# The samples' steps of a two-branch mixer as a chain of their own, with a distance behind each step

## The chip, the cores and the metric

The kernel runs on one core of a Trainium2 chip. The metric is the device time of one execution in microseconds (us). Lower is better. Each time quoted is a median of runs, or one profiled execution where that is said.

The engines are named as in the profile: PE (matrix multiplications), DVE and ACT (elementwise work), POOL, and SP, which issues most of the loads.

## The reference

One layer of a hybrid decoder is computed for a prompt of 1024 tokens and for 8 samples of one token each. They share the weights.

```python
h = rmsnorm(x, norm_gain)
q, k, v, gla_g, a_lr, u, pool_g, xq, xg, merge = split(h @ w_in)
# A: gated linear attention, 4 heads (dk 128, dv 256), chunks of 64, per-head rmsnorm
br_gla  = rmsnorm(gla_chunked(q, k, v, log_sigmoid(a_lr @ w_a2 + b_a) / 16, S0)) * silu(gla_g)
# B: trailing means over 2, 4, 8 and 16 rows, minus the row, linear map of each group, scale
br_pool = multiscale_pool(u, hist) * silu(pool_g)
# C: cross attention of 4 heads (256 wide) into 256 memory tokens
br_x    = cross_attn(xq, mem_k, mem_v) * silu(xg)
merged  = sum_n sigmoid(merge_n) * (branch_n @ w_branch_n)
y       = rmsnorm(x + merged @ w_out, final_gain)
```

For the prompt the memory keys and values come from `mem @ w_mk` and `mem @ w_mv`, and the attention state starts at zero. For each of the 8 samples the keys, the values, the attention state (128 x 256 per head) and the last 15 pooling rows are read from their own caches. Everything is float32, so a large product is split into a high and a low part and made of three matmuls (`mm3`).

## The kernel before

**The large product.** `h @ w_in` is cut into 40 pairs of column blocks, and each pair is computed by seven products of half-size blocks. One call of `run_product` is such a product: 24 matmuls of 128x258 into `px` banks of PSUM. `seq` is the list of the 280 products, and the text numbers them from 1. `prepare` makes the weights' operands (names `a11`, `a12`, `a22`, `s1` to `s4`, each with an `h` and an `l` half) three products ahead: ACT writes the high half (L221), DVE the low half (L222), and DVE also makes sums of raw blocks (`ws<-raw`, L293). The raw blocks are loaded by SP (L284).

**The fill.** After each product `emit` calls `fill`, which adds steps of other work to the same queues. A `Stream` hands out steps of a generator so that the work done, in units written in the `yield`s, keeps up with a line from its first to its last slot. A slot number rises by 2 with each product. The first stream (`mix`) holds the cross attention and then the gated linear attention, from product 15 to 179; the second (`pool_steps`) the pooling, up to product 249.

**Two kinds of steps.** The long sequences (the prompt) of the cross attention: `cross_memory` (M) transposes a head's keys; `cross_scores` (S) makes scores, a maximum, exponentials and a scaling; `cross_weights` (W) transposes the weights and splits them; `cross_values` (V) multiplies by the values. Of the linear attention: `gla_gates` (GG, a long chain on ACT and DVE), `gla_within` (GW, whose result is split into `akvh` and `akvl`), `gla_recur` (R, L867 its last matmul) and `gla_out` (GO, L896).

The samples have generators of their own. `cross_sample` for each head: `cross_rows` transposes the queries and writes them to DRAM; `fetch` loads two samples' keys (`kc`) and their query, spread over all partitions (`qb`); DVE multiplies and sums them (L683, four per fetch, four fetches); the scores `sc` are transposed (L695), softmax, transposed again (L707, copied to `pm`, L708); then two halves of values (`vc`) are loaded and multiplied (L721), and the result transposed (L731). `gla_sample` for each head: rows, gates, two halves of states (`s0`, `vb`) that are fetched, updated, stored and multiplied (L952), and a normalised result (L967).

In the kernel before each sample generator is drawn from inside the long sequences' generator (`yield next(samples, 0)`) at fixed places: five offers per chunk of the cross attention, four per chunk of the linear attention. A small number in a `yield` (0.5) is there to use up an offer.

**What fixes the order.** PE and SP run in the order in which the code issues instructions. On ACT, DVE and POOL a scheduler places them when the kernel is built; on the chip each engine then runs in that fixed order. Steps of a fill use two PSUM banks (`PZ`, tile `pz`) in turn: a step that takes a bank waits until whatever reads the step before the last has finished. `V` is a ring of four buffers for the samples' loads, and one key fetch takes three of them.

Of the kernel before, what the change touches and what calls it, by code (L numbers as in the profile page):

```python
# [9 lines left out]
F32 = mybir.dt.float32  # L10
# [5 lines left out]
ALU = mybir.AluOpType  # L16
# [20 lines left out]
NR = 14  # L37
WORK_A, WORK_B = 493.0, 108.0
WINDOWS = (2, 4, 8, 16)
# [8 lines left out]
def trunk_kernel(ctx: ExitStack, tc: tile.TileContext,  # L48
# [589 lines left out]
    def cross_values(h, c):  # L638
# [9 lines left out]
        nc.gpsimd.dma_start(out=mix_chunk(2, h, c), in_=g)  # L648

    def cross_rows(h):  # L650

        xs = tiny(16, "xs").rearrange("p (i b) -> p i b", i=2)
        nc.vector.tensor_scalar(xs, smp_of(S_XQ + 2 * h, 2), 1.0 / 16.0, None, op0=ALU.mult)
        t = PZ()
        for i in range(2):
            nc.tensor.transpose(t[:NS, i * P:(i + 1) * P], xs[:, i], ident)
        qn = R([DV], name="qn")
        nc.scalar.activation(qn[:NS], t[:NS, :DV], AF.Copy)
        nc.gpsimd.dma_start(out=xq_scr[h], in_=qn[:NS])

    def cross_sample(h):

        if h == 0:
            cross_rows(0)
# [11 lines left out]
        kcs, qb = fetch(0)  # L676
        yield 0.5
        yield 0.5
        for b2 in range(4):
            for bb in range(2):  # L680
                b, kc = 2 * b2 + bb, kcs[bb]
                for a in range(2):
                    nc.vector.tensor_tensor_reduce(kc[:, a, :], kc[:, a, :], qb[:, bb, :],  # L683
                                                   scale=1.0, scalar=0.0, op0=ALU.mult, op1=ALU.add,
                                                   accum_out=sc[:, a * NS + b:a * NS + b + 1])
# [6 lines left out]
        yield 0.5  # L692
        t = PZ()
# [8 lines left out]
        nc.vector.tensor_scalar(p, p, sm, None, op0=ALU.mult)  # L702
        yield 1.2
        yield 0.5
        t = PZ()
# [7 lines left out]
        vc = own_values(0)  # L713
        yield 1.2
        yield 0.5
        cs = R([2, DV], name="cs")
        for i in range(2):
            t = PZ()
            for a in range(2):
                for j in range(4):  # L720
                    nc.tensor.matmul(t[32 * j:32 * j + 32, :DV], lhsT=pm[:, a, 4 * i + j, :], rhs=vc[j][:, a, :],  # L721
                                     start=a == 0, stop=a == 1)
            nc.scalar.activation(cs[:, i], t[:, :DV], AF.Copy)
            vc = own_values(1) if i == 0 else None
            yield 1.2
            yield 0.5
            yield 0.5
        t = PZ()
# [3 lines left out]
        for d in range(2):  # L732
            nc.vector.tensor_copy(perm8(brs[2][:, 2 * h + d]), column0(t, d))
        yield 1.2

    def cross_steps():
# [12 lines left out]

        samples = chain_of(cross_sample(h) for h in range(NH))  # L750
        cross_load(0)
        cross_memory(0)
        cross_fetch(0, 0)
        yield 2
        cross_queries(0, 0)
        cross_fetch(0, 1)
        for s in range(16 + 2):
            if s < 16:
                scores(s)
                yield 3  # L760
                if s + 1 < 16:
                    cross_queries(*divmod(s + 1, 4))
# [9 lines left out]
            if s >= 1:  # L772
                yield next(samples, 0)
            if s % 4 == 3 and s < 15:
                memory(s + 1)
                yield 2
            if 0 <= s - 1 < 16:
                weights(s - 1)
                yield 1.7
            for _ in range(3):  # L780
                if s >= 1:
                    yield next(samples, 0)
        yield from samples

    def chain_of(gens):
        for g in gens:
            yield from g

# [121 lines left out]
    def gla_sample(h):  # L910

        if h == 0:
            gla_rows(0)
            yield 1
        t = PZ()
# [5 lines left out]
        nc.vector.tensor_scalar(qm[:, :, 0], smp_of(S_Q + h)[:, 0], DK ** -0.5, None, op0=ALU.mult)  # L921
        yield 2
        ks = smp_of(S_K + h)[:, 0]
# [17 lines left out]
        for i in range(2):  # L941
            fetched = [fetch(4 * i + b0) for b0 in (0, 2)]
            yield 1
            yield 0.5
            s0 = []
            for b0 in (0, 2):
                s0.append(states(4 * i + b0, *fetched[b0 // 2]))
                yield 1.5
            yield 0.5
            t = PZ()  # L950
# [4 lines left out]
            nc.scalar.activation(t[:, :DV], t[:, :DV], AF.Square, accum_out=sq[:, i:i + 1])  # L955
            yield 1
# [5 lines left out]
        yield 1  # L962
        yield 0.5
        t = PZ()
# [6 lines left out]
        yield 1.2  # L971

    def gla_steps():
        samples = chain_of(gla_sample(h) for h in range(NH))
        N = 16
        gla_load(0, 0)
        gla_load(0, 1)
        gla_gates(0, 0)
        gla_values(0, 0)
        yield 5  # L980
        for n in range(N + 1):
            h, c = divmod(n, 4)
            ph, pc = divmod(n - 1, 4)
            if n + 1 < N:
                gla_gates(*divmod(n + 1, 4))
                yield 5
            if n < N:
                gla_within(h, 2 * c)
                yield 2
            if n > 0:  # L990
                gla_recur(ph, 2 * pc + 1)
                yield 2
                yield next(samples, 0)
            if n < N:
                gla_within(h, 2 * c + 1)
                yield 2
                yield next(samples, 0)
# [5 lines left out]
                yield 2  # L1003
            if n > 0:
                gla_out(ph, pc)
                yield 2
            for _ in range(2):
                if n >= 1:
                    yield next(samples, 0)
        yield from samples  # L1010

# [3 lines left out]
    def pool_steps():  # L1015
# [5 lines left out]

        fetched = group_fetch(0)
        for g, w in enumerate(WINDOWS):
            raw, hist = fetched
# [15 lines left out]
            nc.gpsimd.dma_start(out=o_pool_s[:, HIST - 1, g * DV:(g + 1) * DV], in_=hr[:NS])  # L1040
            yield 3
            diffs, us_ = {}, {}
# [60 lines left out]
            yield 3 + g  # L1103
            for c in range(4):
# [4 lines left out]
                mixed(c)  # L1109
                yield 4 + g if c < 3 else 2  # L1110
            t = PZ()
# [4 lines left out]
            nc.gpsimd.dma_start(out=o_pool_p[:, g * DV:(g + 1) * DV], in_=hr[:HIST])  # L1116
            yield 1

# [3 lines left out]
    def mix():  # L1122
        yield from cross_steps()
        yield from gla_steps()

    class Stream:


        def __init__(self, steps, work, first, last):
            self.steps, self.work, self.first, self.last, self.done, self.over = steps, work, first, last, 0, False  # L1130

        def run(self, slot):
            while self.done < self.work * (slot - self.first) / (self.last - self.first):
                cost = next(self.steps, None)
                if cost is None:
                    self.over = True
                    break
                self.done += cost

        def rest(self):  # L1140
            self.done += sum(self.steps)
# [3 lines left out]
    state = {"slot": 0}  # L1145

    def fill():

        s = state["slot"] = state["slot"] + 2
        next(memory, None)  # L1150
# [272 lines left out]
```

## Time and profile before

| | |
|---|---|
| median of 3 runs | 1486.27 us (1485.35 to 1486.29) |
| the profiled execution | 1486.76 us, span 1485.1 us |
| mean granted clock of PE | 0.99 |
| PE busy | 1449.9 us, 98% of the span |
| DVE busy | 880.6 us, 59% |
| ACT busy | 679.1 us, 46% |

The span runs from the first to the last instruction of the profile; the execution's time adds 1.7 us around it. A group of instructions is shown as line, engine, operation, output tile <- input tiles, shape and count. A bracket "[1.96 <-ACT xqsh L224]" behind an instruction says that its engine stood idle for 1.96 us before it and that ACT's `xqsh` of line 224 ended that. "PEclk" is the share of full speed that PE's clock was granted.

### The profile page before, as it was taken

To read this page: it belongs to the slowest core of one execution; us is meant where nothing else is said; L and a number is where in the kernel's file an instruction comes from. 1 tells how busy PE (TensorE), PEld (TensorE's weight loads), DVE (VectorE), ACT (ScalarE), POOL (GpSimd) and SP (SyncE) were. 2 spreads that over 40 slices of the span, in tenths; PEclk is the share of its full clock that TensorE was granted. 3 is DMA by queue.
4 is the path that set the end of the run, shared out by engine and by line. 5 is a ranking of instruction groups with operands and counts; after the bars stand their busy time and mean duration, and the time that the engine had idled before them with its cause. 6 is when DMAs were issued, how large, how long until landed. Compare 5 with 4: busy or idle time off the path is not lost.

```text
span 1485.1 us, 28245 instructions
## 1 busy us (share of the span) xinstructions
PE 1449.9 (98%) x10881; PEld 1386.6 (93%) x10881; DVE 880.6 (59%) x2020; ACT 679.1 (46%) x1564; POOL 160.1 (11%) x297
## 2 busy tenths in 40 slices
PE   7999999999999999999999999999999999999997
PEld 6798999989899999999989999999999999999786
DVE  5824757555577666666756578685672434554435
ACT  5623444344466665655654444444472332333212
POOL 3121101011111111110111110110010000000000
PEclk9999999999999999999999999999999999999999
DMA  8443566555545354553444455554595677632502
GB/s 297 153 166 128 186 212 201 182 196 178 195 145 173 108 185 146 172 159 125 160 162 134 155 183 165 165 190 145 190 302 160 223 251 248 226 100 93 199 29 86
DMA packets 181714, 255.25 MB, mean 172 GB/s; under 512 B 20412, under 2 KB 134740, under 8 KB 181572
## 3 DMA queue, kind: packets, MB, share of 16 engines
q1 hardware_dynamic: 159772, 179.61, 39.1%
q0 software_dynamic: 21664, 73.59, 13.1%
q8 instruction: 85, 1.39, 0.4%
q14 instruction: 49, 0.40, 0.1%
q10 hardware_dynamic: 144, 0.26, 0.0%
HBM read 176.27 MB, written 77.59 MB: 171 GB/s over the span
## 4 chain that ended last, share of the span: by engine, by line
PE 87%; DMA 5%; DVE 4%; ACT 2%; issue 1%; SPq 0%; DVEq 0%; POOLq 0%; ACTq 0%
PE px L240 24%; PE px L241 24%; PE px L242 24%; PE pz L391 3%; DMA qb<-xqs 2%; PE pz L240 2%; PE pz L242 2%; PE pz L241 2%; DMA raw<-in_w_in_dram 1%; DVE kc L683 1%; DMA x<-in_x_prompt_dram 1%; PE pz L867 1%; PE px L428 1%; PE pz L849 1%; DMA vc<-in_cache_mem_v_dram 1%
## 5 line engine op out<-in xcount | busy, mean ns | idle before, releaser
L240 PE MATMUL px<-bh,wbh 128*128 128x384 f32 (+1 forms) x576 | 184.2, 320 | 0.0
L241 PE MATMUL px<-bl,wbh 128*128 128x384 f32 (+1 forms) x576 | 184.1, 320 | 0.0
L242 PE MATMUL px<-bh,wbl 128*128 128x384 f32 (+1 forms) x576 | 184.0, 319 | 0.0
L482 ACT ACTIVATE r<-px 128x258 f32<-128x258 f32 x240 | 90.1, 377 | 44.3 <-PE px L242 42.9
L241 PEld LDWEIGHTS px<-bl,wbh 128*128 128x128 f32 x576 | 108.4, 188 | 0.0
L242 PEld LDWEIGHTS px<-bh,wbl 128*128 128x128 f32 x576 | 108.3, 188 | 0.0
L240 PEld LDWEIGHTS px<-bh,wbh 128*128 128x128 f32 x576 | 108.2, 188 | 0.0
L240 PE MATMUL px<-ot,s2h 128*128 128x258 f32 x320 | 93.4, 292 | 0.0
L240 PE MATMUL px<-o,a12h 128*128 128x258 f32 x320 | 93.3, 292 | 0.0
L240 PE MATMUL px<-ot,a22h 128*128 128x258 f32 x320 | 93.2, 291 | 0.0
L240 PE MATMUL px<-o,s4h 128*128 128x258 f32 x320 | 92.9, 290 | 0.3 <-DVE c L547 0.3
L240 PE MATMUL px<-ot,s1h 128*128 128x258 f32 x320 | 93.1, 291 | 0.0
L240 PE MATMUL px<-o,a11h 128*128 128x258 f32 x320 | 92.9, 290 | 0.0
L240 PE MATMUL px<-ot,s3h 128*128 128x258 f32 x320 | 92.7, 290 | 0.0
L242 PE MATMUL px<-ot,s2l 128*128 128x258 f32 x320 | 91.4, 286 | 0.0
L241 PE MATMUL px<-o,a12h 128*128 128x258 f32 x320 | 91.2, 285 | 0.0
L242 PE MATMUL px<-o,a12l 128*128 128x258 f32 x320 | 91.0, 284 | 0.0
L241 PE MATMUL px<-ot,s2h 128*128 128x258 f32 x320 | 91.0, 284 | 0.0
L241 PE MATMUL px<-ot,a22h 128*128 128x258 f32 x320 | 91.0, 284 | 0.0
L242 PE MATMUL px<-o,a11l 128*128 128x258 f32 x320 | 90.2, 282 | 0.8 <-DVE a11l L222 0.8
L242 PE MATMUL px<-ot,a22l 128*128 128x258 f32 x320 | 90.8, 284 | 0.0
L242 PE MATMUL px<-ot,s1l 128*128 128x258 f32 x320 | 90.7, 284 | 0.0
(457 smaller groups left out, 4577.5 us busy)
## 6 DMA issues: line engine op xcount, KB each, us to landing
raw<-in_w_in_dram SPq DMA_DIRECT2D x80, 512.0 KB, 3.9
msc<-c POOLq DMA_DIRECT2D x24, 516.0 KB, 4.4
brsc<-c POOLq DMA_DIRECT2D x24, 516.0 KB, 4.3
sig<-msc SPq DMA_DIRECT2D x24, 516.0 KB, 6.0
mix<-mixsc SPq DMA_DIRECT2D x48, 256.0 KB, 4.5
brr<-brsc SPq DMA_DIRECT2D x48, 256.0 KB, 5.4
wbr<-in_w_branch_dram SPq DMA_DIRECT2D x24, 512.0 KB, 6.2
acc<-sig POOLq DMA_DIRECT2D x16, 516.0 KB, 5.2
```

Of the source, the lines that this page charges most:

```text
L240: nc.tensor.matmul(out, lhsT=lh, rhs=rh, start=start, stop=False, skip_group_check=more)
L241: nc.tensor.matmul(out, lhsT=lh, rhs=rl, start=False, stop=False, skip_group_check=more)
L242: nc.tensor.matmul(out, lhsT=ll, rhs=rh, start=False, stop=stop, skip_group_check=more)
L391: nc.tensor.matmul(t[:, :DV], lhsT=memT[k // 2][:, k % 2, a * P:(a + 1) * P], rhs=raw[k // 2][:, k % 2], start=k == 0, stop=k == NK - 1)
L428: nc.tensor.transpose(t[:, j * P:(j + 1) * P], xt[j][:, k * P:(k + 1) * P], ident)
L482: nc.scalar.activation(r, acc[c][:, :QT], AF.Copy)
L683: nc.vector.tensor_tensor_reduce(kc[:, a, :], kc[:, a, :], qb[:, bb, :], scale=1.0, scalar=0.0, op0=ALU.mult, op1=ALU.add, accum_out=sc[:, ...
L849: nc.tensor.matmul(t[0:64, 0:P], lhsT=ki[:, 0:64], rhs=qi, start=True, stop=True)
L867: nc.tensor.matmul(to, lhsT=kiqi[:, 1, cs], rhs=st, start=False, stop=True)
```

## The change

- The samples' chain becomes an object, `Paced`, made once from all eight generators (four heads of cross attention, then four of the linear attention). `mix` offers it a place after every step of the long sequences, and draws what is left at the end.
- Every `yield` now gives two numbers: the work, and a distance. Behind a long step the distance is counted in products before the stream's next step (`Stream.ready`). Behind a sample's step it is 0, 1 or 2 and becomes 0, 2 or 3 slots before the chain's next step (`Paced.ready`); since slots rise by 2, that is no, one or two products. The yields of 0.5 are gone, merged into their neighbours.
- `Stream.run` starts no further step once two PSUM banks have been taken in this fill (`count["pz"]`).
- In `cross_sample` the scaling of the queries is a step of its own (`cross_scaled`), with a tile `xsq` of its own, ahead of `cross_rows`.
- In `cross_steps` the first scores are a fill of their own, two products after the first `cross_memory`; the first loads of the linear attention are issued at s = 15 and its first gates at s = 16, inside the cross attention. In `gla_steps` the last R and in `pool_steps` the first steps get a distance.
- `WORK_A` is 497 instead of 493, for the changed sum of the work.

The core of the diff:

```diff
+    count = {"pz": 0, "slot": 0, "rest": False}
     def PZ():
+        count["pz"] += 1
...
         kcs, qb = fetch(0)
-        yield 0.5
-        yield 0.5
+        yield 0.5, 2
         for b2 in range(4):
...
             if b2 < 3:
                 kcs, qb = fetch(b2 + 1)
-                yield 1.2
+                yield 2.2, 2
             elif h + 1 < NH:
+                cross_scaled(h + 1)
+                yield 1, 1
                 cross_rows(h + 1)
-            yield 1
-        yield 0.5
+        yield 1, 1
...
-        yield 1.2
-        yield 0.5
+        yield 1.7, 2
...
         cross_fetch(0, 0)
-        yield 2
         cross_queries(0, 0)
         cross_fetch(0, 1)
+        yield 2, 2
         for s in range(16 + 2):
             if s < 16:
                 scores(s)
-                yield 3
+                yield 3, int(s < 2)
...
-            if s >= 1:
-                yield next(samples, 0)
             if 0 <= s - 2:
                 values(s - 2)
-                yield 1.7
+                yield 1.7, 0
...
+    class Paced:
+        def __init__(self, gens):
+            self.gen, self.ready, self.over = (v for g in gens for v in g), 0, False
+        def step(self):
+            if self.over or (count["slot"] < self.ready and not count["rest"]):
+                return 0, 0
+            v = next(self.gen, None)
+            if v is None:
+                self.over = True
+                return 0, 0
+            self.ready = count["slot"] + (0, 2, 3)[v[1]]
+            return v[0], 0
...
     def mix():
-        yield from cross_steps()
-        yield from gla_steps()
+        for steps in (cross_steps(), gla_steps()):
+            for v in steps:
+                yield v
+                yield samples.step()
+        while not samples.over:
+            yield samples.step()[0], 1
...
         def run(self, slot):
-            while self.done < self.work * (slot - self.first) / (self.last - self.first):
-                cost = next(self.steps, None)
+            used = count["pz"]
+            while (self.done < self.work * (slot - self.first) / (self.last - self.first)
+                   and slot >= self.ready and count["pz"] < used + 2):
+                v = next(self.steps, None)
...
-                self.done += cost
+                self.done += v[0]
+                self.ready = slot + 2 * v[1]
```

Three places show how the instructions move. Lines of the changed kernel are 3 to 12 higher than those of the kernel before (a step's L601 is its L604); `px` rows are the products, `pz` rows the fill's steps.

PE at product 15, the start of the cross attention, before: M's transposes (`mkv`), then the first S (`mkTh` are the keys, `xqsh` and `xq` the two halves of the queries).

```order
L241 MATMUL px<-ot_933,a22h 128x258
L242 MATMUL px<-ot_932,a22l 128x258
L601 MATMUL pz<-ident,mkv 128x128 x4
L240 MATMUL pz<-mkTh,xqsh 128x256
L241 MATMUL pz<-mkTl,xqsh 128x256
L242 MATMUL pz<-mkTh,xq 128x256
```

The same place in the changed kernel:

```order
L244 MATMUL px<-ot_933,a22h 128x258
L245 MATMUL px<-ot_932,a22l 128x258
L604 MATMUL pz<-ident,mkv 128x128 x4
L243 MATMUL px<-o_502,a12h 128x258
L244 MATMUL px<-o_503,a12h 128x258
L245 MATMUL px<-o_502,a12l 128x258
```

Two products (16 and 17) now stand between M and the first S.

DVE where the fourth head's keys are split (`mkTl`, `mkv`), before: the key products `kc` of the samples' third head stand around the split.

```order
L222 TENSOR_TENSOR a12l<-raw,a12h 128x512
L222 TENSOR_TENSOR s2l<-ws,s2h 128x512
L683 ISA kc,sc<-kc,qb 128x256
L683 ISA sc 128x1
L222 TENSOR_TENSOR mkTl<-pz,mkTh 128x512
L222 TENSOR_TENSOR mkv<-mkv,mvsh 128x512
L556 TENSOR_TENSOR c_3628<-px,r_3426 128x258
```

The same split in the changed kernel:

```order
L708 RECIPROCAL sm<-sm 8x1
L709 TENSOR_SCALAR ps<-ps,sm 8x256
L225 TENSOR_TENSOR s3l<-ws,s3h 128x512
L296 TENSOR_TENSOR ws<-raw 128x512
L225 TENSOR_TENSOR mkTl<-pz,mkTh 128x512
L225 TENSOR_TENSOR mkv<-mkv,mvsh 128x512
L533 TENSOR_TENSOR c_3373<-px,r_3231 128x258
```

No key products stand near it any more; the samples are at their second head's softmax there.

PE at product 177, the end of the linear attention, before: a sample's multiplication by its states, then the last GO, one product after the last R.

```order
L241 MATMUL px<-o_507,a12h 128x258
L242 MATMUL px<-o_506,a12l 128x258
L952 MATMUL pz<-s_9808,pm 32x256 x2
L952 MATMUL pz<-s_9812,pm 32x256 x2
L896 MATMUL pz<-ident,on 128x128 x4
L240 MATMUL px<-ot_655,s2h 128x258
```

The last GO in the changed kernel, at product 179, two products after the last R:

```order
L244 MATMUL px<-ot_707,s1h 128x258
L245 MATMUL px<-ot_706,s1l 128x258
L908 MATMUL pz<-ident,on 128x128 x4
L243 MATMUL px<-ot_773,s3h 128x258
L244 MATMUL px<-ot_774,s3h 128x258
```

No sample's step is left here; the samples end at product 165.

More of the change, by code (lines that the diff above doesn't have):

```diff
@@ L37 @@
 NR = 14
-WORK_A, WORK_B = 493.0, 108.0
+WORK_A, WORK_B = 497.0, 108.0
 WINDOWS = (2, 4, 8, 16)
@@ L648, in cross_values, with cross_scaled @@
         nc.gpsimd.dma_start(out=mix_chunk(2, h, c), in_=g)
+    def cross_scaled(h):
+        xs = wk.tile([P, 16], F32, tag="xsq", name="xsq", bufs=2).rearrange("p (i b) -> p i b", i=2)
+        nc.vector.tensor_scalar(xs, smp_of(S_XQ + 2 * h, 2), 1.0 / 16.0, None, op0=ALU.mult)
+        cross["xs", h] = xs
     def cross_rows(h):
-        xs = tiny(16, "xs").rearrange("p (i b) -> p i b", i=2)
-        nc.vector.tensor_scalar(xs, smp_of(S_XQ + 2 * h, 2), 1.0 / 16.0, None, op0=ALU.mult)
+        xs = cross["xs", h]
         t = PZ()
@@ L663, in cross_sample @@
         if h == 0:
+            cross_scaled(0)
+            yield 1, 1
             cross_rows(0)
-            yield 1.2
-            yield 0.5
-            yield 0.5
+            yield 1.2, 2
         sc = wk.tile([P, 16], F32, tag="sc", name="sc", bufs=2)
@@ L713, in cross_sample @@
         vc = own_values(0)
-        yield 1.2
-        yield 0.5
+        yield 1.7, 2
         cs = R([2, DV], name="cs")
@@ L724, in cross_sample @@
             vc = own_values(1) if i == 0 else None
-            yield 1.2
-            yield 0.5
-            yield 0.5
+            yield 2.2, 2
         t = PZ()
@@ L733, in cross_sample @@
             nc.vector.tensor_copy(perm8(brs[2][:, 2 * h + d]), column0(t, d))
-        yield 1.2
+        yield 1.2, 0
     def cross_steps():
@@ L748, in values @@
             cross_values(n // 4, n % 4)
-        samples = chain_of(cross_sample(h) for h in range(NH))
         cross_load(0)
@@ L766, in cross_steps @@
                 cross_load(s // 4 + 1)
-            if s >= 1:
-                yield next(samples, 0)
             if 0 <= s - 2:
                 values(s - 2)
-                yield 1.7
-            if s >= 1:
-                yield next(samples, 0)
+                yield 1.7, 0
             if s % 4 == 3 and s < 15:
                 memory(s + 1)
-                yield 2
+                yield 2, 0
+            if s == 15:
+                gla_load(0, 0)
+                gla_load(0, 1)
+            if s == 16:
+                gla_gates(0, 0)
+                yield 5, 0
             if 0 <= s - 1 < 16:
                 weights(s - 1)
[L779 to L787, printed above, removed]
+                yield 1.7, int(s >= 15)
+    class Paced:
[10 more added lines that the diff above has]
+            return v[0], 0
     gla = {}
@@ L913, in gla_sample @@
             gla_rows(0)
-            yield 1
+            yield 1, 1
         t = PZ()
@@ L921, in gla_sample @@
         nc.vector.tensor_scalar(qm[:, :, 0], smp_of(S_Q + h)[:, 0], DK ** -0.5, None, op0=ALU.mult)
-        yield 2
+        yield 2, 1
         ks = smp_of(S_K + h)[:, 0]
@@ L942, in gla_sample @@
             fetched = [fetch(4 * i + b0) for b0 in (0, 2)]
-            yield 1
-            yield 0.5
+            yield 1.5, 2
             s0 = []
@@ L947, in gla_sample @@
                 s0.append(states(4 * i + b0, *fetched[b0 // 2]))
-                yield 1.5
-            yield 0.5
+                yield 2, 1
             t = PZ()
@@ L955, in gla_sample @@
             nc.scalar.activation(t[:, :DV], t[:, :DV], AF.Square, accum_out=sq[:, i:i + 1])
-            yield 1
+            yield 1, 0
         if h + 1 < NH:
@@ L961, in gla_sample @@
             nc.scalar.activation(os_[:, i], os_[:, i], AF.Copy, scale=r[:, i:i + 1])
-        yield 1
-        yield 0.5
+        yield 1.5, 2
         t = PZ()
@@ L970, in gla_sample @@
                                     op0=ALU.mult)
-        yield 1.2
+        yield 1.2, 0
+    samples = Paced([f(h) for f in (cross_sample, gla_sample) for h in range(NH)])
     def gla_steps():
-        samples = chain_of(gla_sample(h) for h in range(NH))
         N = 16
-        gla_load(0, 0)
-        gla_load(0, 1)
-        gla_gates(0, 0)
         gla_values(0, 0)
-        yield 5
         for n in range(N + 1):
@@ L985, in gla_steps @@
                 gla_gates(*divmod(n + 1, 4))
-                yield 5
+                yield 5, 0
             if n < N:
                 gla_within(h, 2 * c)
-                yield 2
+                yield 2, 0
             if n > 0:
                 gla_recur(ph, 2 * pc + 1)
-                yield 2
-                yield next(samples, 0)
+                yield 2, 0 if n < N else 2
             if n < N:
                 gla_within(h, 2 * c + 1)
-                yield 2
-                yield next(samples, 0)
+                yield 2, 0
                 if n + 2 < N:
@@ L1002, in gla_steps @@
                 gla_recur(h, 2 * c)
-                yield 2
+                yield 2, 0
             if n > 0:
                 gla_out(ph, pc)
[L1006 to L1010, printed above, removed]
+                yield 2, 0
     HALO = 16
@@ L1022, in pool_steps @@
         fetched = group_fetch(0)
+        yield (0.5), 2
         for g, w in enumerate(WINDOWS):
@@ L1109, in pool_steps @@
                 mixed(c)
-                yield 4 + g if c < 3 else 2
+                yield (4 + g if c < 3 else 2), 0
             t = PZ()
@@ L1116, in pool_steps @@
             nc.gpsimd.dma_start(out=o_pool_p[:, g * DV:(g + 1) * DV], in_=hr[:HIST])
-            yield 1
+            yield (1), 0
     memory = mem_units()
     def mix():
-        yield from cross_steps()
-        yield from gla_steps()
+        for steps in (cross_steps(), gla_steps()):
[4 more added lines that the diff above has]
+            yield samples.step()[0], 1
     class Stream:
         def __init__(self, steps, work, first, last):
-            self.steps, self.work, self.first, self.last, self.done, self.over = steps, work, first, last, 0, False
+            self.steps, self.work, self.first, self.last = steps, work, first, last
+            self.done, self.ready, self.over = 0, 0, False
         def run(self, slot):
-            while self.done < self.work * (slot - self.first) / (self.last - self.first):
-                cost = next(self.steps, None)
-                if cost is None:
+            used = count["pz"]
+            while (self.done < self.work * (slot - self.first) / (self.last - self.first)
+                   and slot >= self.ready and count["pz"] < used + 2):
+                v = next(self.steps, None)
+                if v is None:
                     self.over = True
                     break
-                self.done += cost
+                self.done += v[0]
+                self.ready = slot + 2 * v[1]
         def rest(self):
-            self.done += sum(self.steps)
+            count["rest"] = True
+            self.done += sum(v[0] for v in self.steps)
+            count["rest"] = False
             assert abs(self.done - self.work) < 9, self.done
     streams = [Stream(mix(), WORK_A, 14 * 2, int(14 * 25.5)), Stream(pool_steps(), WORK_B, int(14 * 25.5), 14 * 36 - 6)]
-    state = {"slot": 0}
     def fill():
-        s = state["slot"] = state["slot"] + 2
+        s = count["slot"] = count["slot"] + 2
         next(memory, None)
```

8 lines of the change are left out of this document (3 added, 5 removed).

## The prediction

> **What bounds the kernel now.** I read the page first, its busy shares and its slices.
>
> ```profile
> span 1485.1 us, 28245 instructions
> PE 1449.9 (98%) x10881; PEld 1386.6 (93%) x10881; DVE 880.6 (59%) x2020; ACT 679.1 (46%) x1564; POOL 160.1 (11%) x297
> PE   7999999999999999999999999999999999999997
> ```
>
> PE is busy for 1449.9 of 1485.1 us. The change adds and removes no matmul, so at most the other 35.2 us, and the time in which PE runs slowly, can move. Next come the windows by stage, to see where the idle time lies: the cross attention runs from 130 us, the linear attention from about 400, the pooling from 790.
>
> ```profile
> 130.00:400.00 270.00, 259.94 (x2164) 249.63 (x2163) 161.90 (x421) 115.08 (x280) 29.75 (x56) 0.99 0.59 191
> 400.00:790.00 390.00, 386.66 (x3160) 368.88 (x3159) 262.95 (x671) 238.88 (x650) 49.76 (x84) 1.00 0.47 153
> 790.00:1090.00 300.00, 300.00 (x2507) 299.79 (x2507) 213.46 (x461) 140.62 (x299) 32.53 (x57) 1.00 0.54 174
> ```
>
> After the stretch come PE, PEld, DVE, ACT and POOL busy, then the granted clock. In the pooling PE has no gap: 2507 matmuls in 300 us, 0.120 us each, so a product of 24 lasts 2.87 us. Nothing can be won there. The two stages with the samples' steps hold 10.1 + 3.3 = 13.4 us of idle PE. The rest of the 35.2 us lies in the prologue and the tail, whose code is the same. PE's waits from 130 to 790 us name the idle time:
>
> ```profile
> PE pz L656 <- DVE mkTl L222: 2.8, 1, 2.8
> PE pz L896 <- ACT on L885: 2.2, 1, 2.2
> PE pz L240 <- ACT xqsh L224: 2.0, 1, 2.0
> PE pz L721 <- DMA vc<-in_cache_mem_v_dram: 1.5, 2, 1.1
> PE pz L635 <- ACT xo L647: 1.1, 1, 1.1
> PE pz L707 <- DVE ps L702: 1.0, 1, 1.0
> PE pz L952 <- issue: 0.8, 1, 0.8
> PE pz L242 <- DVE xq L225: 0.6, 2, 0.4
> PE pz L695 <- DVE mkTl L222: 0.6, 1, 0.6
> PE pz L721 <- DVE pm L708: 0.3, 1, 0.3
> PE pz L240 <- ACT p L75: 0.2, 1, 0.2
> ```
>
> Columns: who waited for whom, sum, times, longest. Thirteen waits, 13.1 us. All stand at a `pz` instruction, a step of the fill; no product waits. The long ones cost more than their own length, as the timeline and windows of PE alone show:
>
> ```profile
> 136.88 0.39 PE L240 MATMUL pz<-mkTh,xqsh 128*128 128x256 f32 x1 [1.96 <-ACT xqsh L224]
> ...
> 138.61:142.02 3.41, 3.41 (x19) 0.50 0.91 340
> 309.27:312.69 3.42, 3.42 (x18) 0.50 0.01 2
> 776.90:780.31 3.41, 3.41 (x18) 0.50 0.22 77
> 780.31:783.72 3.41, 3.41 (x30) 1.00 0.00 0
> ```
>
> Within 2 us of each of the three longest waits (they end at 136.9, 308.2 and 775.6 us; the rows of the last two stand below) PE's clock is granted at 0.50 for 3.41 us, and 18 matmuls run where 30 do in the next window: 3.41 x 12/30 = 1.4 us lost each time, 4.1 us together. No other stretch from 130 to 790 us is below full clock. So 13.1 + 4.1 = **17.2 us** is all that this change can win.
>
> [...]
>
> **The change, wait by wait.** From the order of both kernels I counted the products between a waiting step and the step that it needs.
>
> | wait (us) | needs | before | now |
> |---|---|---|---|
> | first S (2.0 + 0.6) | M and its loads | 0 | 2 |
> | sample scores, L695 (0.6) | bank of M | 1 | no sample step |
> | sample rows, L656 (2.8) | bank of M | 1 | no sample step |
> | second values, L721 (1.5) | their loads | 1 | 2 or 3 |
> | softmax, L707 (1.0) | sample scores | 1 | 2 |
> | first values, L721 (0.3) | `pm` | 0 | 2 |
> | W, L635 (1.1) | bank, third in one fill | 0 | never three |
> | states, L952 (0.8) | bank of GW | 1 | other neighbours |
> | GO, L896 (2.2) | last R | 1 | 2 |
>
> Start of the cross attention: two products are 5.7 us where the wait lacked 2.0, so 2.6 us of waits and 1.4 of clock go.
>
> The wait of 2.8 us is DVE's. It works in order:
>
> ```profile
> DVE kc L683 <- DMA qb<-xqs: 23.6, 11, 3.8
> 294.40 0.43 DVE L683 CUSTOM_DVE_ANT_0 kc<-kc,qb 128x256 f32<-128x256 f32 x1 [2.21 <-DMA qb<-xqs]
> 307.12 0.43 DVE L683 CUSTOM_DVE_ANT_0 kc<-kc,qb 128x256 f32<-128x256 f32 x1 [3.75 <-DMA qb<-xqs]
> 307.48 0.69 DVE L222 TENSOR_TENSOR mkTl<-pz,mkTh 128x512 fp32r<-128x512 f32 x1
> 308.22 0.38 PE L656 MATMUL pz<-ident,xs 128*8 128x128 f32 x2 [2.81 <-DVE mkTl L222]
> ```
>
> DVE stood at a key product for 3.75 us until `qb` landed, `mkTl` was queued behind it, and PE needed M's bank. Two fetch rounds lie from 294.40 to 307.12, so 6.4 us is the chain's own pace: DVE's four key products free `V`, then SP loads. The fetches of this head stood after products 50, 51, 52 and 54. Now they are at least two products apart, 5.7 us and the steps between (an S or V is 12 matmuls, 1.4 us; one or two of them), so 7 to 8.5 us against 6.4. The loads then land before DVE comes to them. 0.6 + 2.8 + 1.4 us go.
>
> Short links (values, softmax, `pm`): a product and its neighbours more is 2.9 us against waits of 0.3 to 1.1. 2.8 us go. Third bank in a fill: 1.1, and the 0.2 of a V behind exponentials. The bank of GW:
>
> ```profile
> 590.13 0.32 PE L849 MATMUL pz<-kiqi 128*64 128x128 f32 x1
> 595.09 0.68 DVE L222 TENSOR_TENSOR akvl<-pz,akvh 128x512 fp32r<-128x512 f32 x1
> 595.87 0.64 PE L952 MATMUL pz<-s,pm 128*32 128x256 f32 x8 [0.80 <-issue]
> ```
>
> The bank came free when DVE had split GW's result, 5.6 us after GW. Last GO:
>
> ```profile
> 769.30 0.59 PE L867 MATMUL pz<-st,kiqi 128*128 128x256 f32 x2
> 773.15 0.69 DVE L293 TENSOR_TENSOR ws<-raw 128x512 f32<-128x512 f32 x1 [2.73 <-DMA raw<-in_w_in_dram]
> 775.57 0.95 PE L896 MATMUL pz<-ident,on 128*128 128x128 f32 x4 [2.22 <-ACT on L885]
> ```
>
> R ends at 769.9, GO can start at 775.6: 5.7 us, of which DVE spent 2.73 on a late raw block. Two products are 5.74 us, so the wait goes even if the block is late again: 2.2 + 1.4.
>
> What is late next, each bounded below by 0:
> - Second values of the last head: products 94 and 96 with only GG between, 5.9 us. The chain shows the first half (x16) and the landing of the second's loads for two heads:
>
> ```profile
> 198.47 1.00 PE pz L721 x16
> 200.97 4.48 DMA vc<-in_cache_mem_v_dram
> ...
> 384.09 1.00 PE pz L721 x16
> 386.60 5.28 DMA vc<-in_cache_mem_v_dram
> ```
>
>   From 199.5 to 205.4 us, 6.0, and from 385.1 to 391.9, 6.8. I take 0.5 (to 1.0).
>
> - Scores of the last head stand one product behind their last key products (89, 90). Nearest: the 0.6 of L695. I take 0.6 (to 2.8).
> - R one product behind a GW whose bank it takes (products 92, 98, 100, 113, 131). Nearest: the 0.8 above, for one such place of many. I take 0.8 (to 2.4).
> - W one product behind M, in M's bank (products 38, 51). I take 0.6, the milder of the two waits before (to 2.8 + 1.4).
> - A late raw block. The distance doesn't touch DVE's waits for them; of 14, one stood ahead of the wait for GO.
>
> ```profile
> DVE ws L293 <- DMA raw<-in_w_in_dram: 18.3, 14, 2.7
> ```
>
> I take 0.7 (to 2.2 + 1.4). Together 3.2 us, at most 14.
>
> At nothing: `cross_scaled` (its DVE instruction stands earlier), the early gates at products 65 and 69 (long ahead of GW at 71 and 76), and the pooling's new distances. The cover for all is PE's queue of products, and were it gone, each would show as a `pz` wait. SP passes the same loads in a new order; its raw loads stand behind sample loads that wait for `V`, as before.
>
> Sum: 17.2 - 3.2 = 14.0. The profiled execution took 1486.76 (span 1485.1 and 1.7 around it): 1472.8. It stands 0.5 above the median of 1486.27, so **1472.3**.
>
> **Rivals.**
> - Half of it comes back (0.20). Other steps get the tight places, as the last head's and the five R; sums of 5 to 14 us of new waits, each over 2 us with its 1.4 of clock. For it: the two stages stay as full (DVE 161.9 of 270 and 263.0 of 390 us). Against it: before, some twenty banks of GW were taken again one product later (counted in the order), and one step waited, for 0.8. Time 1479.
> - No change (0.09). The four new terms at their upper ends, 14 us: 1483.
> - Slower (0.05). The third head's key products move from products 51 to 56 to products 60 to 67, beside the first GG, and the last head's from 67 to 71 to 82 to 89, into DVE's fuller stage. If `qb` is late there, DVE stands still, and akv and GG behind it, 2.8 + 1.4 = 4.2 us at each of the eight rounds of these heads. It decides from five such stops on, 21 us against 17.2: 1490. Against it: two products plus R and GW are more than the 6.4 us of a round.
> - The half clock isn't due to the waits (0.04): 13.1 - 3.2 = 9.9 are won, 1476.4. Against it: it follows the three longest waits and none of the shorter. [...]
>
> **How the numbers follow.** My forecast has 0.62 and reaches from 1468.5 (with nothing new late the sum is 1469.1) to 1476.5. Up to 1481 most of the first rival and the fourth are inside, 0.8 in all. A change under 0.2%, 3 us, can't be told from none here. Faster holds the forecast, the first and the fourth: 0.86; same 0.09; slower 0.05.
>
> **What would show it.** PE's waits from 130 to 790 us should sum to some 3 us, with no wait over 1.5 us and no window at 0.50 there; the first S, L656, L635 and the last GO should be gone from them. DVE's wait for `qb` should fall from 23.6 to under 8 us. I am wrong if new `pz` waits of over 2 us appear (the last head's scores, R behind GW, W behind M), or if DVE still waits for `qb`.

## The result and the profile after

| | before | changed |
|---|---|---|
| median of 6 runs each | 1485.81 us (1482.21 to 1488.04) | 1476.75 us (1473.9 to 1478.1) |
| ratio | | 0.9941, 95% interval 0.9923 to 0.9959 |
| profiled execution | 1486.76, span 1485.1 | 1478.1, span 1476.4 |

The change gains 9 us, 0.6%. The forecast was 14. The profiled execution of the changed kernel is the slowest of its six. The page of the changed kernel, its first lines:

```profile
span 1476.4 us, 28260 instructions
PE 1446.0 (98%) x10881; PEld 1384.1 (94%) x10881; DVE 881.4 (60%) x2020; ACT 679.7 (46%) x1564; POOL 159.8 (11%) x297
PE   7999999999999999999999999999999999999997
```

The starts of products 15 and 180 on PE, from the timelines of the kernel before (first two rows) and of the changed one, tell which stage moved:

```profile
131.44 0.28 PE L240 MATMUL px<-ot,a22h 128*128 128x258 f32 x1
784.59 0.37 PE L240 MATMUL px<-ot,s3h 128*128 128x258 f32 x1
```

```profile
130.54 0.28 PE L243 MATMUL px<-ot,a22h 128*128 128x258 f32 x1
774.89 0.36 PE L243 MATMUL px<-ot,s3h 128*128 128x258 f32 x1
```

The two stages with the samples' steps took 653.15 us and take 644.35: 8.8 us less, which is all of the span's 8.7. PE's waits in them (130 to 790 us; who waited for whom, sum, times, longest), changed kernel:

```profile
PE pz L823 <- DMA alc<-als: 3.3, 1, 3.3
PE pz L908 <- DVE akvl L225: 2.5, 1, 2.5
PE pz L243 <- ACT xqsh L227: 1.2, 1, 1.2
PE pz L861 <- ACT pz L893: 1.1, 1, 1.1
PE px L243 <- DVE c L559: 0.7, 1, 0.7
PE pz L245 <- DVE xq L228: 0.2, 1, 0.2
PE pz L823 <- ACT pz L893: 0.2, 1, 0.2
```

Seven waits, 9.2 us, where thirteen with 13.1 us stood. None stands at a sample's step: the waits of M's bank (L656 and L695 of before), of values, softmax, W, states and the last GO are gone. The new ones stand at the long sequences' own steps, and one at a product (`px`). The windows of PE alone (stretch, PE busy, granted clock, DMA share, GB/s) show two stretches near half clock behind the two longest waits, where before there were three:

```profile
376.44:379.85 3.41, 3.41 (x15) 0.53 0.61 192
509.56:512.97 3.41, 3.41 (x19) 0.53 0.19 77
```

**Each long wait in the timeline.** The first gates of the linear attention (L823) waited for `alc`. The first two rows are SP's, which issued the loads, the third is PE's:

```profile
369.30 2.97 SPq L584 DMA_DIRECT2D vc<-in_cache_mem_v_dram  x4
372.32 0.46 SPq L814 DMA_DIRECT2D alc<-als  x1
...
376.38 0.97 PE L823 MATMUL pz<-alc,w 128*128 128x256 f32 x2 [3.29 <-DMA alc<-als]
```

The issue order puts four loads of the samples' values ahead of `alc`. They had to wait until PE had released their buffers, and only then, at 372.32, was the load issued that PE needed at 373.1.

The GO of L908 waited for a PSUM bank that GW had filled, and with it for DVE's split of GW's result:

```profile
505.30 0.48 DVE L947 SCALAR_TENSOR_TENSOR s<-vb,smp,s 128x256 f32<-128x256 f32 x1 [3.07 <-DMA vb<-vs]
...
507.77 0.69 DVE L225 TENSOR_TENSOR akvl<-pz,akvh 128x512 fp32r<-128x512 f32 x1 [0.32 <-ACT akvh L224]
...
508.61 0.63 PE L908 MATMUL pz<-ident,on 128*128 128x128 f32 x4 [2.48 <-DVE akvl L225]
```

The split stood behind a sample's state update (L947), for whose load `vb` DVE stopped 3.07 us. The change didn't remove such stops. DVE's waits for the samples' loads in the whole span, changed kernel:

```profile
DVE s L947 <- DMA vb<-vs: 17.6, 9, 5.6
DVE kc L689 <- DMA qb<-xqs: 14.1, 10, 2.4
```

Before they were 8.6 (the same line was L935) and 23.6: the stops for `qb` fell, but not below 8 us as forecast, and those for `vb` doubled.

### The profile page after: what moved, and what is told of

Its sections match the earlier page's. It is cut to its first block, busy times and chain, and to the rows that moved or that the text cites. A ratio compares the mean times of both kernels' runs of the same rounds, so it can differ in the third digit from the quotient of the medians.

```text
span 1476.4 us, 28260 instructions
## 1 busy us (share of the span) xinstructions
PE 1446.0 (98%) x10881; PEld 1384.1 (94%) x10881; DVE 881.4 (60%) x2020; ACT 679.7 (46%) x1564; POOL 159.8 (11%) x297
## 4 chain that ended last, share of the span: by engine, by line
PE 91%; DMA 3%; DVE 3%; ACT 2%; issue 1%; SPq 1%; POOLq 0%; POOL 0%; DVEq 0%; ACTq 0%
PE px L243 25%; PE px L244 25%; PE px L245 25%; PE pz L394 3%; PE pz L243 2%; PE pz L245 2%; PE pz L244 2%; DMA vb<-vs 1%; DMA x<-in_x_prompt_dram 1%; PE px L431 1%; PE pz L879 1%; PE pz L861 1%; PE pz L726 1%; PE pz L823 0%; PE pz L863 0%
## 5 line engine op out<-in xcount | busy, mean ns | idle before, releaser
L243 PE MATMUL px<-ot,s1h 128*128 128x258 f32 x320 | 93.7, 293 | 0.0
L243 PE MATMUL px<-ot,s3h 128*128 128x258 f32 x320 | 93.5, 292 | 0.1
L243 PE MATMUL px<-ot,s2h 128*128 128x258 f32 x320 | 92.2, 288 | 0.0
L243 PE MATMUL px<-ot,a22h 128*128 128x258 f32 x320 | 91.8, 287 | 0.0
L244 PE MATMUL px<-ot,s1h 128*128 128x258 f32 x320 | 91.4, 286 | 0.0
L244 PE MATMUL px<-ot,s3h 128*128 128x258 f32 x320 | 91.1, 285 | 0.0
L245 PE MATMUL px<-ot,s3l 128*128 128x258 f32 x320 | 91.0, 284 | 0.0
L245 PE MATMUL px<-o,s4l 128*128 128x258 f32 x320 | 90.5, 283 | 0.0
```

The source lines that it names most:

```text
L243: nc.tensor.matmul(out, lhsT=lh, rhs=rh, start=start, stop=False, skip_group_check=more)
L244: nc.tensor.matmul(out, lhsT=lh, rhs=rl, start=False, stop=False, skip_group_check=more)
L245: nc.tensor.matmul(out, lhsT=ll, rhs=rh, start=False, stop=stop, skip_group_check=more)
```

## The experiments

All were timed in three rounds against the kernel before on the same chip (median 1486.4 us in each of the three groups). "Changed kernel" is the one with the whole change.

### What the parts of the change are worth

**The changed kernel once more**, to see whether its waits return.

> The changed kernel once more, to see which of its waits are a matter of its order and which of the moment. If the order sets them (theory), PE waits again some 3 us at L823 for alc, some 2 to 2.5 us at L908, 1.2 us at L243 for xqsh, and 1477 us come out. If they are chance (rival), other places wait, the sum from 130 to 790 us still being 7 to 11 us.

1475.74 us, ratio 0.9933 (0.9912 to 0.9955). The same places wait again: L823 for `alc` 3.5, L908 for `akvl` 1.4, L861 1.1, the second S 1.2, a product 1.4. Two others came, a V for `pTl` 1.1 and a product for `r` 0.5. So the order sets the main places, and chance their length and some small waits.

**No distance in the samples' chain.**

```diff
-            self.ready = count["slot"] + (0, 2, 3)[v[1]]
+            self.ready = count["slot"] + (0, 0, 0)[v[1]]
```

> The changed kernel with every distance of the samples' chain set to 0: the chain still is offered a place after each step, and two banks per fill still are the limit. Theory (the distance keeps DVE from standing at loads that are under way): DVE's wait for qb and vb rises from 32 us to over 45, PE's waits from 130 to 790 us from 9 to over 14 us, 4 to 8 us slower than the changed kernel, 1482. Rival (the new places and the limit of two banks do it): within 1.5 us of the changed kernel.

1485.0 us, 0.9985 (0.9971 to 0.9999). With the chain as an object and all else in place, but no distances, 1.4 us are left of the gain. PE's waits sum to 13.5 us, as before the change, and DVE's for `qb` to 28.9. The edit does more than shorten the distances, though: the samples' steps then take more of the fills early, and the long sequences come later (the gates that waited for `alc` at 376.4 us stand at 431.9). So the run shows what the distances are worth with the order that they make, and doesn't part the two.

**No cap on the banks of one fill.**

```diff
-                   and slot >= self.ready and count["pz"] < used + 2):
+                   and slot >= self.ready and count["pz"] < used + 99):
```

> The changed kernel without the limit of two banks per fill, distances kept. Theory (a third bank in a fill waits for readers of the same fill, as the 1.1 us at L635 before): one or two waits of about 1 us come back, 1 to 3 us slower than the changed kernel. Rival (with the distances there is rarely a third bank, so the limit has nothing to do): within 1 us.

1481.3 us, 0.9961 (0.9946 to 0.9976). The changed kernel's waits stay, and two more steps of the fill wait, a V 1.3 us for its operand `pTh` and an S 1.2 us behind the split `pTl`. The median lies 5.6 us above that of the changed kernel's second run, but the two profiled executions differ by only 1.6 and the intervals overlap a little. So the cap probably helps, by some 2 to 5 us; I can't say more closely.

**No distance at the last R.**

```diff
-                yield 2, 0 if n < N else 2
+                yield 2, 0
```

> The changed kernel without the distance behind the last R, so the last GO comes one product after it. Theory (R to GO takes 5.7 us where a raw block is late, 3.0 us where not; a product is 2.87 us): a wait of 0.2 to 2.3 us at L908 comes back, with a window at 0.50 if it is long, 0.5 to 3 us slower than the changed kernel. Rival: no wait, within 0.5 us.

1479.3 us, 0.9956 (0.9939 to 0.9972). Of the 2.2 us of before, this row is what came back:

```profile
773.02 0.95 PE L908 MATMUL pz<-ident,on 128*128 128x128 f32 x4 [0.42 <-ACT on L897]
```

The interval overlaps that of the changed kernel, so the distance's own worth isn't shown by the time. The wait for the last GO was mostly gone without it: no raw block came late there this time.

**No distance at the first S.**

```diff
-        yield 2, 2
+        yield 2, 0
...
-                yield 3, int(s < 2)
+                yield 3, 0
```

> The changed kernel with no distance behind the first M and the first two S: M, the first S and the second S go back to one product or none apart. Theory (each wait at a fill's step is paid in full, with 1.4 us of clock behind a long one): the wait of 2.0 us for xqsh and the window at 0.50 come back and the later wait of 1.2 us goes, so 2 to 3 us slower than the changed kernel, 1479. Rival (the wait only moves on to the next step that needs the same loads): within 1 us.

1471.73 us, 0.9903 (0.9876 to 0.993): not slower as expected, but with a median 4 us lower (the intervals overlap a little). The first S waits again. In the profiled execution little else does, but that is the fastest of the four (1466.04 us; the others took 1469.82 to 1474.61):

```profile
PE pz L243 <- ACT xqsh L227: 2.0, 1, 2.0
PE pz L243 <- DVE rq L255: 1.0, 1, 1.0
PE pz L245 <- DVE xq L228: 0.5, 1, 0.5
```

Without the two products at the start all later steps of both chains stand earlier, so other steps meet. `alc` was issued at 360.42 us, 15.7 us ahead of its gates, as the four loads of values ahead of it found their buffers free by 359; no GO stood behind a late `vb`. Whether the distance itself is harmful or this is chance had to be told apart with those other waits gone; that is done at the end.

### Taking the new waits away

**The loads of the gates earlier**, at the beginning of a round of the linear attention instead of its end.

```diff
+            if n + 2 < N:
+                gla_load(*divmod(n + 2, 4))
             if n + 1 < N:
                 gla_gates(*divmod(n + 1, 4))
...
-                if n + 2 < N:
-                    gla_load(*divmod(n + 2, 4))
                 if n + 1 < N:
                     gla_values(*divmod(n + 1, 4))
```

> The changed kernel with the loads of the next chunk's gates (alc, kq) issued at the start of an iteration of the linear attention instead of just ahead of the sample steps of its end. PE's order is unchanged. Theory (at product 73 these loads stand on SP behind four value loads of the samples that wait for the multiplication before them, and the gates follow one product later): the wait of 3.3 us at L823 and the window at 0.50 behind it go, 3 to 5 us faster than the changed kernel, 1472. Rival (the loads are late because of the transfers under way, not of the queue): the wait stays.

1472.79 us, 0.99 (0.9877 to 0.9923), some 3 us below the changed kernel, with intervals that just overlap. PE's order is that of the changed kernel, and the wait at L823 is gone (first row). But elsewhere a GO now waits 3.84 us for its bank, which ACT was still to read (L893). ACT stood 5.45 us ahead of that reading, at a state's update (L946) whose state `s` was late; DVE stood 5.33 us for the `vb` of the same update:

```profile
375.39 0.59 PE L823 MATMUL pz<-alc,w 128*128 128x256 f32 x2
...
621.70 0.91 ACT L946 ACTIVATE s<-s,as 128x256 f32<-128x256 f32 x2 [5.45 <-DMA s<-in_state_gla_dram]
...
622.55 0.88 DVE L947 SCALAR_TENSOR_TENSOR s<-vb,smp,s 128x256 f32<-128x256 f32 x2 [5.33 <-DMA vb<-vs]
...
622.77 0.37 ACT L893 ACTIVATE pz<-pz 128x256 f32<-128x256 f32 x1
...
623.31 0.66 PE L908 MATMUL pz<-ident,on 128*128 128x128 f32 x4 [3.84 <-ACT pz L893]
```

In the changed kernel ACT stood 4.50 us for `s` and DVE 5.61 us for `vb` at about the same place (630 us). There ACT had read the bank ahead of its stop (L893 at 624.52), and only a product lost 0.7 us, to DVE. So the stop was there all along; what it costs PE depends on what stands behind it on the engine.

**The second S's queries earlier.** In the changed kernel they were split in the S's own fill, behind an operand of the large product.

```diff
+                if s == 0:
+                    cross_queries(0, 1)
+                    cross_fetch(0, 2)
                 yield 3, int(s < 2)
-                if s + 1 < 16:
+                if 0 < s and s + 1 < 16:
...
-                if s + 2 < 16:
+                if 0 < s and s + 2 < 16:
```

> The changed kernel with the second chunk's queries split in the fill of the first S instead of in the fill of the second S. PE's order is unchanged. Theory (the split is issued in the same fill as its consumer and waits on ACT behind a weights' half that needs PE): the 1.2 + 0.2 us at the second S go, 1 to 2 us faster than the changed kernel. Rival (the load of the queries is late): it stays.

1476.19 us, 0.9925 (0.9904 to 0.9945). The second S no longer waits, but the time can't be told from the changed kernel's: the intervals are wider than the 1.2 us to be won, and `pTl` made PE wait 2.0 us elsewhere (1.1 in the second run of the changed kernel).

**Holding DVE's and ACT's instructions for the samples.** `last["lo"]` and `last["hi"]` are DVE's and ACT's latest split instruction at the time of issue. `tc.issue_after` makes the scheduler put an instruction behind a given one.

```diff
+                    with tc.issue_after(last["lo"].ins):
                         nc.vector.tensor_tensor_reduce(kc[:, a, :], ...)    # the key product
...
+                with tc.issue_after(last["hi"].ins), tc.issue_after(last["lo"].ins):
                     nc.scalar.activation(s0[:, i], ...)                     # the state update
                     nc.vector.scalar_tensor_tensor(s0[:, i], vb[:, i], ...)
```

> The changed kernel with the states' updates and the key products held on ACT and DVE behind the last split of weights that was issued ahead of them; PE's and SP's order unchanged. Theory (the distance is kept on PE and SP, but the scheduler places these instructions on DVE as early as it believes their loads to be there, so DVE stands at them and GW's split or a product's sum waits behind): DVE's wait for vb falls from 15 to 18 us to under 8, the waits at L908, L861 and of a product for c (2.5 to 4 us and a window at 0.50) go, 3 to 5 us faster than the changed kernel. Rival (DVE's stops cost PE nothing, other work is late): within 1.5 us.

1473.08 us, 0.9907 (0.9888 to 0.9926), some 3 us below the changed kernel, with intervals that just overlap. DVE's wait for `vb` is gone from the list, ACT's for `s` too (12.7 us in the changed kernel), and that for `qb` is down from 14.1 to this:

```profile
DVE kc L690 <- DMA qb<-xqs: 4.9, 5, 1.9
```

At the GO of 508.6 us the order on DVE has turned round, without a stop:

```profile
504.19 0.68 DVE L225 TENSOR_TENSOR akvl<-pz,akvh 128x512 fp32r<-128x512 f32 x1
...
506.63 0.87 DVE L949 SCALAR_TENSOR_TENSOR s<-vb,smp,s 128x256 f32<-128x256 f32 x2
```

Three of PE's waits went with it (L908, L861, the product's). The same three are gone in the run with the earlier loads, where the order on DVE ahead of this GO is still the old one, but the stop for `vb` lasts only 1.05 us. So for L908 the rows show the cause in both ways; for L861, with no stop for a load in the 7 us ahead of it in the changed kernel, it stays open. `alc` (3.5) and the second S stay, as they should, and one wait of 1.9 for `mkTl` came.

**All three together.** The edits above in one kernel.

> The three edits together. Theory: PE waits under 2 us from 130 to 790 us, no window at 0.50, 1468 us. Rival (each wait that goes lets another come): 1472 or more.

1465.9 us, 0.9859 (0.9841 to 0.9877): the fastest of all, about 20.5 us ahead of the kernel before and 10 ahead of the changed one. By themselves the three edits gained some 3, 0 and 3 us: in each of those runs another wait had come or stayed (3.8 us at a GO, 3.1 and 3.5 at L823). Its page, its only wait of PE from 130 to 790 us, and that stretch of PE alone:

```profile
span 1464.2 us, 28252 instructions
PE 1441.5 (98%) x10881; PEld 1381.4 (94%) x10881; DVE 880.8 (60%) x2020; ACT 681.9 (47%) x1564; POOL 159.9 (11%) x297
```

```profile
PE pz L638 <- DVE mkTl L225: 0.6, 1, 0.6
```

```profile
130.00:790.00 660.00, 659.23 (x5501) 1.00 0.54 173
```

### With the waits gone: the distances again

**The three edits, no distance at the start** (as e1 above, in the last kernel).

> All three edits, but no distance behind the first M and the first S's. Theory (the earlier run without this distance was faster only because the whole chain moved away from the late loads at L823 and the late states): with those gone the start's own wait shows, 2.0 + 0.5 us at the first S, so 2 to 4 us slower than the three edits with the distance, 1468 to 1470. Rival (the start's distance itself costs time): as fast or faster, 1464 to 1466.

1470.94 us, 0.9902 (0.9886 to 0.9918): 5 us slower than with it. The waits sum to 3.9 us, and behind the first S stands a half-clock window again:

```profile
136.26 0.49 PE L243 MATMUL pz<-mkTh,xqsh 128*128 128x256 f32 x1 [1.96 <-ACT xqsh L227]
...
136.44:139.85 3.41, 3.11 (x14) 0.51 0.77 289
```

Of the 3.9 us, 1.6 stand at later steps. So the distance at the start is worth having here. That the earlier trial gained by the shift of all later steps fits its trace, without the waits at L823 and L908, but is not shown by a run of its own.

**The three edits, no distance in the samples' chain** (the edit of the second experiment).

> All three edits, but every distance of the samples' chain 0. Theory (distance and holding are two different things: the distance gives the loads their time, the holding keeps DVE from standing at them): short links and loads under way wait again on PE and DVE, 8 to 12 us slower than the three edits, 1475 or more. Rival (holding alone is enough): within 3 us, under 1469.

1480.12 us, 0.9967 (0.9957 to 0.9978), 14.2 us slower than with distances. PE's longest waits are at two V's, behind the exponentials `p` that ACT makes late, and at a sample's transposed softmax:

```profile
PE pz L243 <- ACT p L75: 4.8, 2, 2.6
PE pz L714 <- DVE ps L710: 1.7, 1, 1.7
```

**The kernel before, with the holding alone.** The same `issue_after` lines, none of the change.

> The kernel before with nothing but the holding of the states' updates and key products. Theory: DVE's wait for qb falls from 23.6 to under 12 us and the wait of 2.8 us at L656 with its 1.4 us of clock goes, while the waits at the first S, the short links and the last GO stay: 3 to 6 us faster than before, 1481. Rival (holding alone gives what the distance gave): 1476 or less.

1482.95 us, 0.9977 (0.9961 to 0.9993). The wait of 2.8 us at L656 is gone, as DVE no longer stops ahead of `mkTl`. DVE's wait for `qb` fell from 23.6 to 15.2 only, more than expected. Holding without distances is worth 3 us, distances without holding 9 to 10, both with the two earlier issues 20.5.

## Why the prediction was right and wrong

**Right: what was to be won, and by what.** The waits of the table went with the distances. Take the distances out and the waits are back, other ones of the same sum (13.5 us) and the same time (1485.0). That the start is worth 2.6 + 1.4 us was near: 5 us when measured by itself, with 1.6 us of waits at later steps among them. The time lies in the wide range, up to 1481, but 0.25 us beyond the end of the forecast's own, 1476.5.

**Wrong: the term "what is late next".** I took 3.2 us, at most 14. Measured: 9.2 us of new waits and two half-clock windows, 2.8 us, so 12.0, near the upper end. The places were wrong too. Of the five that I named, none waits in the changed kernel (one, W in M's bank, did with the holding, 1.9 us). By the sum of before, 17.2 - 12.0 = 5.2 us would be the gain; 8.8 were measured in that stage, so the two errors partly cancel. That the time came as near as it did is in part luck.

- *The gates' loads (3.3 + 1.4).* I put the early gates at product 65 and 69 at nothing, said nothing of the next ones at product 74, and wrote that "SP passes the same loads in a new order". I didn't follow that order to the first use of each load: at product 74 `alc` stands behind four loads that wait for PE. The earlier issue removed the wait.
- *DVE and ACT at the states (2.5 + 1.4, 1.1 and 0.7).* I costed R behind GW, and had DVE standing at `qb` in a rival, but took it that a distance in the code is a distance on DVE. It isn't: the scheduler places DVE's and ACT's instructions itself when the kernel is built, and put a state update ahead of the split that PE needed. In the trace before, 8.6 us of stops for `vb` stood in the list of DVE's waits, unread. Holding removed the stops and those waits of PE; only for the 1.1 at L861 is the link not shown.
- *The second S (1.2).* I gave the first S two products and forgot that the next S has its own split.

**Wrong: the ceiling.** "17.2 us is all that this change can win" counted idle time and clock. From the changed kernel to the one with all three edits, 8.6 us of waits and 2.8 us of clock went, 11.4, but the stage went from 644.35 to 631.07 us, 13.3. From before to there it is 16.6 named and 22.1 measured. About 5 us more lie inside PE's busy time. Part of it is the way in which a wait is counted. The matmuls overlap in these traces: a product's matmul is shown with 0.28 us, but the next one starts 0.12 us behind its start. A wait counts only from the end of the matmul before it, as at the wait for `alc` in the changed kernel, 3.56 us from start to start with 3.29 named:

```profile
372.82 0.28 PE L245 MATMUL px<-ot,s1l 128*128 128x258 f32 x1
376.38 0.97 PE L823 MATMUL pz<-alc,w 128*128 128x256 f32 x2 [3.29 <-DMA alc<-als]
```

By these rows some 0.16 us more (0.28 - 0.12) are lost at each wait. Another part is the instruction at a wait. The first S's is 0.39 us long behind its wait in the trace before; in the kernel with all three edits, without one, it is

```profile
141.01 0.28 PE L243 MATMUL pz<-mkTh,xqsh 128*128 128x256 f32 x1
```

An estimate from these rows, 0.16 + 0.11 us for each wait that went, is 1.6 us of the 1.9 that were missing from the changed kernel to the last (six waits), and 3.2 of the 5.5 from before (twelve). I haven't found the rest row by row; this stays open.

**The half clock.** The rival that it isn't due to waits falls: with all long waits gone no window below full clock is left in the stage (1.00 from 130 to 790 us), and a wait of 1.96 us brought one back (0.51). That the time fell within 0.4 us of that rival's 1476.4 is chance. But my "Within 2 us of each of the three longest waits" was a loose reading. In the kernel before, its half-clock stretches start whole multiples of 3.413 us apart (138.61, 309.27 and 776.90 us, 50 and 187 of them later), and the two in its prologue, from 19.14 and 43.04 us, lie on the same grid, 35 and 28 of them ahead of the first. In the changed kernel the one from 21.65 us lies 104 of them ahead of the one from 376.64 us (the window above, at 0.53, starts 0.2 us early). I laid such a grid on each of the fourteen profiled executions, and took PE's idle time in each window at full clock from 130 to 790 us against the clock of the next window. First two windows with their next of the kernel with the earlier gate loads, then two of the one without distances (PE busy behind the stretch's length; the rest is idle):

```profile
334.57:337.98 3.41, 1.90 (x16) 1.00 0.77 242
337.98:341.39 3.41, 3.25 (x27) 1.00 0.85 263
621.29:624.70 3.41, 1.39 (x12) 1.00 1.03 390
624.70:628.11 3.41, 3.41 (x18) 0.50 0.48 180
```

```profile
345.79:349.20 3.41, 1.71 (x15) 1.00 0.80 275
349.20:352.61 3.41, 3.41 (x19) 0.50 0.22 77
```

| idle in one window of the grid | windows | next window at half clock |
|---|---|---|
| 0.93 to 1.51 us | 28 | 0 |
| 1.67 to 1.91 us | 6 | 3 |
| 1.96 to 3.18 us | 18 | 18 |

With 1.96 us or more idle, 57% of a window, the next one stood at half clock in 18 of 18 cases, with up to 1.51 us in none of 28, and between them in 3 of 6. In these executions the idle time in one window tells the cases apart better than the length of a wait: behind one of 1.70 us that lies whole in a window the next stood at half clock, and the 1.67 us wait of the first of these rows, which ran over the boundary, left 1.51 us in its window and cost no clock. What decides between 1.67 and 1.91 us stays open. The 1.96 us wait in the trial without the distance at the start is such a case. The stretch in its prologue fixes the grid, 1.91 us of the wait lie in one window, and the clock stays full behind it:

```profile
20.89:24.30 3.41, 2.97 (x14) 0.50 1.04 412
130.12:133.53 3.41, 1.50 (x13) 1.00 0.60 168
133.53:136.95 3.42, 2.86 (x21) 1.00 0.94 281
```

**The rivals' chances.** "Half of it comes back" (1479) was nearer in its mechanism than my forecast, and the time lies between the two. At 0.20 I had it too low: the argument against it was a count of banks taken again in the order, and that count says nothing of how late DVE is.

## What to carry to other kernels

In this kernel a distance in the order of issue bound the engines that run in that order, PE and SP. On DVE and ACT, which a scheduler orders, an instruction that needed a load had to be held behind a nearby one as well: unheld, it stopped the queue ahead of work that PE needed (3.07 us of DVE and 2.48 us of PE at the GO of 508.6 us). When steps are moved, follow SP's queue at every load of the other stream that is used soon after its issue. And judge a part of such a change only after the other waits are gone: the same edit lowered the median by 4 us at first, probably by shifting what comes later, and lost 5 us in the clean kernel.

## What the runs showed of the hardware

In these traces a stop of DVE or ACT at a late load (3 to 5.6 us) reached PE through a PSUM bank that the stopped engine was still to read. Where ACT's reading stood ahead of the stop, stops of 4.5 us on ACT and 5.6 on DVE cost PE 0.7 us; where it stood behind, 5.4 us on ACT cost 3.84. And waits of PE cost more than their idle time here: a window at half clock (1.4 us lost in the kernel before, 18 matmuls where 30 run at full clock) stood behind each of the 18 windows of the 3.413 us grid with 1.96 us or more idle, and in these stages about a third came on top of the named waits and windows together (22.1 against 16.6 us).
